# Two transformer blocks in one kernel: other buffers for a small MLP's weights, another instruction for 44 one-column sums, and 128 bytes between two groups of buffers

## The chip, the cores and the metric

The kernel runs on one core of one Trainium2 chip. The metric is the device time of one execution in microseconds. Five engines work beside each other, each on its own list of instructions: TensorE (PE in the rows; its weight loads are PEld), VectorE (DVE), ScalarE (ACT), GpSimd (POOL) and SyncE (SP, which here only issues DMAs).

## The reference, cut to what matters

256 tokens of width 1024, with 256 context tokens, go through two blocks. The first is attention in two forms, modulated by a small adaptive network, followed by a SwiGLU feed-forward with a hidden width of 2816:

```python
def _swiglu(h, w_ffn_in, w_ffn_out):
    gate, up = jnp.split(h @ w_ffn_in, 2, axis=-1)
    return (jax.nn.silu(gate) * up) @ w_ffn_out
...
    h = _modulate(_rmsnorm(new_lat), sh_f, sc_f)          # h * (1 + scale) + shift
    new_lat = new_lat + g_f * _swiglu(h, w_ffn_in, w_ffn_out)
```

The second block adds a state-space mixer (S5) and a sparse attention, merges them by gates, and ends in a squared-ReLU MLP with a hidden width of 4096. Its attention scores the queries against 15 compressed keys, which come out of a small MLP over blocks of 32 tokens (w1 is 2048x128 and w2 128x64, one pair for the keys and one for the values):

```python
def compress_blocks(tok, pe, w1, w2):
    ...
    return jax.nn.gelu(flat @ w1) @ w2
...
    kc = rmsnorm(compress_blocks(kv[0, 0], cmp_pe_k, cmp_wk1, cmp_wk2), k_norm_g[0])
    sc = jnp.einsum('bghqd,bgcd->bghqc', qb, kc) * scale - slopes * dist_c
...
        x = x + jnp.square(jax.nn.relu(h2 @ w_up[l])) @ w_down[l]
```

## The kernel before, in words

**Weights.** The large weights lie in one stream, `in_wseq`, in the order in which they are used. SyncE loads it in granules of 128x2048 fp32 (1 MB) into three buffers with the tag `raw`. ScalarE rounds each half of a granule to fp32r (`hi<-raw`, 128x1024), and VectorE computes what the rounding lost (`lo<-raw,hi`, 128x1024). There are four `hi` and four `lo` buffers. A 128x128 weight then costs three matmuls (`lin`): hi with the rounded activation, hi with its remainder, lo with the rounded activation. That keeps fp32 accuracy.

**Order.** The program is first recorded, instruction by instruction, and then ordered by a list scheduler in the class `Rec`, which keeps one clock per engine and hands out buffers in their order. `Rec.issue` then lays out the buffers in SBUF and writes every instruction; since that is one line, every row of the profile has the line L659 (L660 after the change). Tiles are told apart by their tags: `raw`, `hi`, `lo`; `c` for working tiles (20 of 128x256, made by `c1`, 32 of 128x512, made by `c2`, and 3 of 128x258, `c258`); `col` for a few columns; `xs` for the activations that the matmuls take; `mm`, `s`, `tp`, `v`, `la` for PSUM.

**Feed-forward in** ("ffi" below; the loop over 22 `j`, two `z` each). Each of the 44 lins takes 24 matmuls of 258 columns: 256 tokens, and two columns of the modulation's shift, rounded part and remainder. VectorE scales the PSUM result into a `c258` tile `t` and adds the tile's last column to the one before it, which gives one value per partition. ScalarE uses that of the gate as the bias of Silu, VectorE that of the up branch in the product. In the same stage VectorE and GpSimd compute row sums for the adaptive network (`raw<-raw,k_crow`), and GpSimd builds tables for the S5 mixer (`s5_params`).

**Feed-forward out** ("ffo") is 8 lins of 66 matmuls with 256 columns, whose activations are `c2` tiles.

**Second block.** After the projections come the compression MLP (`tp<-...`, 16 steps for each of keys and values), the S5 steps (`v<-k_cst,c`, `tp<-c,c`), the gate lins, and the scores against the compressed keys (`s<-k_crow,k_kcn`), which need the compression's result `k_kcn`. The compression's weights `w1` are two loads of 1 MB (`in_w` in the rows) into two of the three `raw` buffers, where they stay until the 32 matmuls have read them. At the end stand `up` (32 lins of 24 matmuls) and `down` (8 of 96).

**Addresses.** `Rec.issue` places buffers whose width is a multiple of 128 bytes first, pads the `xs` tiles, then 64 bytes, then all `hi` and `lo` buffers without a gap, then the rest.

Of the kernel before, what the change touches and what calls it, by code (L numbers as in the profile page):

```python
# [15 lines left out]
OP = mybir.AluOpType  # L16
# [338 lines left out]
class Rec:  # L355
# [276 lines left out]
    def issue(self):  # L632
        self.prepare()
        order = self.schedule()

        wide = {}
        for tops in self.tops:
            for r in tops:
                if r.tag in self.bufs and r.tag not in PSTAGS:
                    wide[r.tag] = max(wide.get(r.tag, 0), int(np.prod(r.shape[1:])))  # L640
        lay = [(f"{t}s{k}", w, None) for t, w in wide.items() for k in range(self.bufs[t])]
        lay += [(r.tag, int(np.prod(r.shape[1:])), r) for r in self.fixed]
        mid = [x for x in lay if x[0][:2] in ("hi", "lo")]
        whole = [x for x in lay if x[1] % 32 == 0 and x not in mid]

        small = [[x for x in lay if 0 < x[1] - lo <= 8] for lo in (8, 0)]
        for x in lay:
            if x[0][:2] == "xs":
                whole += [x] + [s.pop() if s else ("k_pad" + x[0], n, None) for s, n in zip(small, (16, 8))]
        rest = [x for x in lay if x not in whole and x not in mid]  # L650
        for tag, w, r in whole + [("k_pad", 16, None)] + mid + rest:
            if r is None:
                self.touch("lay_" + tag, tag, w)
            else:
                r.get()
        val = lambda x: x.get() if isinstance(x, View) else x
        for i in order:
            o = self.ops[i]
            getattr(self.real[o.eng], o.fn)(*[val(x) for x in o.args], **{k: val(x) for k, x in o.kw.items()})  # L659
# [6 lines left out]
def build(tc, nc, A, out):  # L666
    with ExitStack() as ctx:
        with tc.manual_schedule():
            _build(ctx, tc, nc, A, out)


def _build(ctx, tc, nc, A, out):
# [7 lines left out]
    V, ACT, G, PE, SP = (rec.eng(e) for e in ("V", "ACT", "G", "PE", "SP"))  # L680

    def own(pool, name, tag, shape, dt):

        def make():
            t = f"{tag}s{v.root.slot}"
            return pool.tile(shape, dt, tag=t, name=name, bufs=1)
        v = rec.root(tag, shape, dt, make)
        return v

    def T(tag, shape, dt=F32):  # L690
        cnt[0] += 1
        name = f"{tag}_{cnt[0]}"
        return own(sp, name, tag, shape, dt)
# [7 lines left out]
    def PS(tag, shape):  # L701
        cnt[0] += 1
        name = f"{tag}_{cnt[0]}"
        return own(pp, name, tag, shape, F32)
# [4 lines left out]
    def mm2(o, a, b, start, stop):  # L709
        return PE.matmul(o, a, b, start=start, stop=stop, skip_group_check=True)  # L710
# [3 lines left out]
    def PSR(shape, tags):  # L714
        k = rot[tags] = rot.get(tags, -1) + 1
        return PS(tags[k % len(tags)], shape)
# [4 lines left out]
    def c1(dt=F32, n=256):  # L721
        return T("c1", [128, n], dt)

    def c2(dt=F32):
        return T("c2", [128, 512], dt)
# [223 lines left out]
    def lin(o, base, nk, xh, xl, first=0, total=None, k0=0):  # L949

        total = total or nk
        for kc in range(nk):
            wh, wl = wt(base + kc)
            i = first + kc
            h, l = xh(kc), xl(kc)
            mm2(o, wh, h, i == 0, False)
            mm2(o[:, 0:_free(l)], wh, l, False, False)
            mm2(o, wl, h, False, i == total - 1)

    def split(dst_h, dst_l, src):  # L960
        ACT.activation(dst_h, src, AF.Copy)
        V.tensor_tensor(dst_l, src, dst_h.bitcast(F32), OP.subtract)
# [5 lines left out]
    def gemv(i):  # L968
        w = T("raw", [128, 2048])
        SP.dma_start(w, A["ada2"][i])  # L970
        for z in range(2):
            wz = w[:, 1024 * z:1024 * z + 1024]
            o = adc[i // 4][:, 2 * i % 8 + z:2 * i % 8 + z + 1]
            if z in GEMV_POOL[i]:
                G.tensor_tensor(wz, wz, crow, OP.mult)
                ACT.activation(wz, wz, AF.Copy, accum_out=o)
            else:
                V.tensor_tensor_reduce(wz, wz, crow, 1.0, 0.0, OP.mult, OP.add, o)
        if i % 4 == 3:
            o = adc[i // 4]  # L980
            V.tensor_tensor(o, o, col("b_ada", 16 + 2 * i - 6, 8), OP.add)
            if i == 11:
                V.tensor_scalar(o, o, 1.0, None, op0=OP.add)
# [74 lines left out]
    ps = fp[0]  # L1058
# [19 lines left out]
    for m in range(2):  # L1078
        t = c1()
# [7 lines left out]
    for m in range(4):  # L1087
        ps = fp[3 + m]
# [258 lines left out]
    for m in range(8):  # L1347
        if m < 4:
            ps = woa[m // 2][:, m % 2]
        else:  # L1350
            ps = PSR([128, 256], ("s", "v5", "s"))
# [6 lines left out]
                               op0=OP.mult, op1=OP.subtract)  # L1358
# [128 lines left out]
    for j in range(22):  # L1487
        ts = []
        for z in range(2):
            ps = PSR([128, 258], LIN)  # L1490
            lin(ps, BASE["ffi"] + 16 * j + 8 * z, 8, xh_, xl_)
            t = T("c258", [128, 258])
            V.tensor_tensor(t, ps, rsf, OP.mult)
            V.tensor_tensor(t[:, 256:257], t[:, 256:257], t[:, 257:258], OP.add)
            ts.append(t)
        a = c1()
        ACT.activation(a, ts[0][:, 0:256], AF.Silu, bias=ts[0][:, 256:257])
        V.scalar_tensor_tensor(a, ts[1][:, 0:256], ts[1][:, 256:257], a, op0=OP.add, op1=OP.mult)
        h_ = c2(F32R)
        split(h_[:, 0:256], h_[:, 256:512], a)  # L1500
        hid.append(h_)
        if j in (2, 6, 10, 14):
            gemv(12 + j // 4)
        if j == S5P_AT:
            sb2, cp, ca, dd, gd, TB = s5_params()
# [4 lines left out]
    for m in range(8):  # L1510
        ps = PSR([128, 256], LIN)
# [5 lines left out]
                               op0=OP.mult, op1=OP.subtract)  # L1517
# [25 lines left out]
    def lin2(base, tag="mm"):  # L1543
        ps = PS(tag, [128, 256])
        lin(ps, base, 8, xh2, xl2)
        return ps
# [9 lines left out]
    for m in range(4):  # L1556
        ps = lin2(BASE["u"] + 8 * m, UT[m])
# [4 lines left out]
        w_ = table[m]  # L1562
# [83 lines left out]
    TT = []  # L1646
    pe = T("col", [128, 32])
    SP.dma_start(pe, A["pe"])
    for z, nm in enumerate(("k0", "v0")):
        ps = lin2(BASE[nm], IN2[z])  # L1650
# [8 lines left out]
        t = c2().rearrange("p (a b) -> p a b", a=16)  # L1659
# [19 lines left out]
    for z, nm in enumerate(("k1", "k2")):  # L1679
        ps = lin2(BASE[nm], IN2[2 + z])  # L1680
# [31 lines left out]
    for m in range(4):  # L1712
        ps = lin2(BASE["q"] + 8 * m, QT[m])
# [13 lines left out]
    SP.dma_start(w2c, A["w2c"])  # L1727
    kcn, vcn = K("kcn", [128, 32]), K("vcn", [16, 2, 64])
    G.memset(kcn, 0.0)
    w1 = [T("raw", [128, 2048]) for _ in range(2)]  # L1730
    for z in range(2):
        SP.dma_start(w1[z], A["w1"][z])

    ps = PS("tp", [64, 128])
    for l2 in range(16):
        for z in range(2):
            mm2(ps[32 * z:32 * z + 32], TT[z][:, l2], w1[z][:, 128 * l2:128 * l2 + 128], l2 == 0, l2 == 15)
    hd, hx = c1(n=128)[0:64], c1(n=128)[0:64]
    V.tensor_copy(hx, ps)
    gelu_arg(hd, hx)  # L1740
# [28 lines left out]
    for g in range(2):  # L1769
        ps = PS("s", [128, 256])  # L1770
# [3 lines left out]
    for qt in range(2):  # L1774
# [24 lines left out]
        for g in range(2):  # L1799
# [3 lines left out]
            t = c2()  # L1803
# [27 lines left out]
        for kt in range(qt + 1):  # L1831
            for br in range(2):
                n_ += 1
                ts = []
                for g in range(2):
# [3 lines left out]
                    t = c2()  # L1839
# [16 lines left out]
    for q in range(4):  # L1856
        ACT.activation(ys[q], ys[q], AF.Gelu_apprx_tanh)
        t = c2(F32R)
# [9 lines left out]
    for m in range(4):  # L1868
        ps = PSR([128, 256], LIN)
        lin(ps, BASE["glu"] + 4 * m, 4, lambda kc: ygp[kc][:, 0:256], lambda kc: ygp[kc][:, 256:512])  # L1870
        t = c1()
# [9 lines left out]
    for m in range(8):  # L1881
# [9 lines left out]
        t = c2(F32R)  # L1891
# [3 lines left out]
    for m in range(8):  # L1895
        ps = PSR([128, 256], LIN)
# [15 lines left out]
    for j in range(32):  # L1912
        ps = PSR([128, 256], LIN)
# [8 lines left out]
    for m in range(8):  # L1922
        ps = PSR([128, 256], LIN)
        lin(ps, BASE["down"] + 32 * m, 32, lambda kc: hid[kc][:, 0:256], lambda kc: hid[kc][:, 256:512])
        t_ = c1()
        for z in range(2 if m == 7 else 1):
            c = slice(128 * z, 128 * z + 128) if m == 7 else slice(0, 256)
            t = t_.kid((slice(None), c))
# [18 lines left out]
```

## Time and profile before

| | |
|---|---|
| median of 3 runs | 813.47 us (812.05 to 814.28) |
| profiled execution | 813.07 us, its span 811.3 us (1.8 us lie around it) |
| mean granted TensorE clock | 0.976 of full speed |
| busy: PE, DVE, ACT, POOL | 773.4, 586.0, 433.0, 303.5 us |
| chain that ended last | PE 86%, DVE 8%, ACT 2%, DMA 2% |

Busy time says how full an engine is over the whole span. The chain follows the work back from the last instruction, at each step to whatever released it, so its shares tell which engine set the pace, and for how long.

### The profile page before, as it was taken

The page shows a single profiled execution, that of the slowest core. Times are in us where ns is not written, and L with a number is a line of the kernel's source. Part 1 is how long each engine was busy: PE and PEld are TensorE (multiplying, and loading weights), DVE is VectorE, ACT ScalarE, POOL GpSimd, SP SyncE. Part 2 cuts the span into 40 slices and gives each one's busy share as a digit, 9 for nine tenths or more (in the row PEclk, how much of TensorE's full clock was granted, in tenths as well). Part 3 has the DMA queues.
Part 4 walks back from the last instruction along what each step waited for, and adds up shares of the span by engine and source line. Part 5 has one row for each costly group of instructions (what it writes and reads, how often), then busy time and mean ns, then how long its engine had stood idle before and what let it go on. Part 6 is the DMA issues. An engine that isn't in the chain of part 4 may idle for free.

```text
span 811.3 us, 15419 instructions
## 1 busy us (share of the span) xinstructions
PE 773.4 (95%) x6063; PEld 699.5 (86%) x6063; DVE 586.0 (72%) x1156; ACT 433.0 (53%) x790; POOL 303.5 (37%) x320
## 2 busy tenths in 40 slices
PE   5999998999999898899999969999999999999998
PEld 3778775669999798899999857597999999999997
DVE  6678788787998899766676798656688655554552
ACT  6344549877654353465544323666646666643331
POOL 0015255680397999100002566785240333310000
PEclk9999899999999999999999995999999999999999
DMA  8955544435884464465556222033455545555540
GB/s 334 375 178 210 201 155 136 151 119 208 236 279 161 172 212 153 167 232 189 181 190 215 88 104 105 1 134 128 156 178 186 193 173 206 165 201 201 187 170 14
DMA packets 33131, 142.90 MB, mean 176 GB/s; under 512 B 11681, under 2 KB 15137, under 8 KB 16674
## 3 DMA queue, kind: packets, MB, share of 16 engines
q1 hardware_dynamic: 33058, 141.91, 49.8%
q8 instruction: 48, 0.79, 0.4%
q14 instruction: 25, 0.20, 0.1%
HBM read 139.53 MB, written 1.05 MB: 173 GB/s over the span
## 4 chain that ended last, share of the span: by engine, by line
PE 86%; DVE 8%; ACT 2%; DMA 2%; issue 1%; POOL 0%; SPq 0%; DVEq 0%; POOLq 0%
PE mm L659 41%; PE s L659 32%; PE tp L659 6%; DVE c L659 4%; PE la L659 4%; PE v L659 3%; DVE lo L659 2%; ACT c L659 1%; DMA raw<-in_wseq 1%; DVE col L659 1%; DMA raw<-in_ada 1%; ACT hi L659 0%; DMA k_X<-in_x 0%; POOL c L659 0%; DVE k_adc L659 0%
## 5 line engine op out<-in xcount | busy, mean ns | idle before, releaser
L659 DVE TENSOR_TENSOR lo<-raw,hi 128x1024 fp32r<-128x1024 f32 x206 | 258.6, 1258 | 98.7 <-ACT hi L659 97.6
L659 ACT ACTIVATE hi<-raw 128x1024 fp32r<-128x1024 f32 x206 | 215.6, 1050 | 193.5 <-PE mm L659 92.9
L659 PE MATMUL mm<-xs,hi 128*128 128x256 f32 (+1 forms) x992 | 187.9, 288 | 0.8 <-ACT hi L659 0.8
L659 PEld LDWEIGHTS mm<-xs,hi 128*128 128x128 f32 x992 | 156.5, 193 | 6.2 <-issue 4.2
L659 PE MATMUL mm<-c,hi 128*128 128x256 f32 (+1 forms) x744 | 144.3, 292 | 4.6 <-DVE c L659 2.6
L659 PE MATMUL mm<-xs,lo 128*128 128x256 f32 (+1 forms) x496 | 143.2, 289 | 2.6 <-DVE lo L659 2.5
L659 PEld LDWEIGHTS mm<-c,hi 128*128 128x128 f32 x744 | 115.9, 190 | 14.2 <-issue 4.7
L659 PE MATMUL s<-xs,hi 128*128 128x256 f32 (+1 forms) x672 | 124.7, 285 | 2.5 <-ACT hi L659 2.0
L659 PE MATMUL s<-c,hi 128*128 128x256 f32 (+1 forms) x676 | 122.7, 281 | 0.0
L659 PE MATMUL mm<-c,lo 128*128 128x256 f32 (+1 forms) x372 | 107.2, 290 | 1.3 <-DVE lo L659 1.2
L659 PEld LDWEIGHTS s<-xs,hi 128*128 128x128 f32 x672 | 104.3, 190 | 3.8 <-ACT hi L659 3.4
L659 PEld LDWEIGHTS s<-c,hi 128*128 128x128 f32 x676 | 104.0, 188 | 1.4 <-issue 0.4
L659 PEld LDWEIGHTS mm<-xs,lo 128*128 128x128 f32 x496 | 95.9, 194 | 5.1 <-DVE lo L659 4.3
L659 PE MATMUL s<-xs,lo 128*128 128x258 f32 (+1 forms) x336 | 95.9, 285 | 3.9 <-DVE lo L659 3.9
L659 ACT ACTIVATE c<-c 128x256 fp32r<-128x256 f32 (+4 forms) x141 | 61.7, 448 | 67.6 <-DVE c L659 64.5
L659 PE MATMUL s<-c,lo 128*128 128x256 f32 x338 | 95.1, 282 | 0.0
L659 POOL TENSOR_TENSOR raw<-raw,k_crow 128x1024 f32<-128x1024 f32 x18 | 46.3, 2576 | 102.2 <-DMA raw<-in_ada 101.8
L659 DVE TENSOR_TENSOR c<-c,c 128x256 fp32r<-128x256 f32 (+2 forms) x115 | 62.7, 558 | 20.3 <-POOL c L659 15.8
L659 POOL TENSOR_TENSOR c<-c 128x256 f32<-128x256 f32 x40 | 40.7, 1017 | 95.3 <-ACT c L659 81.8
L659 PEld LDWEIGHTS mm<-c,lo 128*128 128x128 f32 x372 | 71.5, 193 | 3.1 <-DVE lo L659 2.0
L659 PEld LDWEIGHTS s<-xs,lo 128*128 128x128 f32 x336 | 64.1, 191 | 4.9 <-DVE lo L659 4.8
L659 PEld LDWEIGHTS s<-c,lo 128*128 128x128 f32 x338 | 64.3, 190 | 0.4
(259 smaller groups left out, 1153.4 us busy)
## 6 DMA issues: line engine op xcount, KB each, us to landing
raw<-in_wseq SPq DMA_DIRECT2D x102, 1024.0 KB, 4.9
raw<-in_ada SPq DMA_DIRECT2D x20, 1024.0 KB, 5.0
tab<-in_ada SPq DMA_DIRECT2D x4, 1024.0 KB, 7.2
raw<-in_w SPq DMA_DIRECT2D x2, 1024.0 KB, 5.0
k_X<-in_x SPq DMA_DIRECT2D x4, 256.0 KB, 4.3
raw<-in_wseq SPq DMA_DIRECT2D x2, 512.0 KB, 7.5
tab<-in_ctx SPq DMA_DIRECT2D x4, 256.0 KB, 10.3
out<-c SPq DMA_DIRECT2D x7, 128.0 KB, 1.7
```

Source lines behind the costliest of these rows:

```text
L659: getattr(self.real[o.eng], o.fn)(*[val(x) for x in o.args], **{k: val(x) for k, x in o.kw.items()})
```

## The change

Three edits. The sum of the two shift columns becomes a `tensor_scalar`, whose second operand is a column read once per partition, in place of a `tensor_tensor` with two tensors. The weights `w1` get eight working tiles of 128x512 (`c2`) and are loaded by eight DMAs of 256 KB. The layout places all `hi` buffers, then 128 bytes of padding, then all `lo` buffers; `hi` stays where it was, and `lo` and all that follows move by 128 bytes.

```diff
@@ Rec.issue
-        mid = [x for x in lay if x[0][:2] in ("hi", "lo")]
+        mid = [x for t in ("hi", "lo") for x in lay if x[0][:2] == t]
+        mid.insert(self.bufs["hi"], ("k_pad2", 32, None))
@@ feed-forward in
             V.tensor_tensor(t, ps, rsf, OP.mult)
-            V.tensor_tensor(t[:, 256:257], t[:, 256:257], t[:, 257:258], OP.add)
+            V.tensor_scalar(t[:, 256:257], t[:, 257:258], t[:, 256:257], None, op0=OP.add)
@@ compression
-    w1 = [T("raw", [128, 2048]) for _ in range(2)]
+    w1 = [[c2() for _ in range(4)] for _ in range(2)]
     for z in range(2):
-        SP.dma_start(w1[z], A["w1"][z])
+        for i, w_ in enumerate(w1[z]):
+            SP.dma_start(w_, A["w1"][z][:, 512 * i:512 * i + 512])
...
-            mm2(ps[32 * z:32 * z + 32], TT[z][:, l2], w1[z][:, 128 * l2:128 * l2 + 128], l2 == 0, l2 == 15)
+            mm2(ps[32 * z:32 * z + 32], TT[z][:, l2], w1[z][l2 // 4][:, 128 * (l2 % 4):128 * (l2 % 4) + 128], l2 == 0, l2 == 15)
```

The scheduler orders the program anew. Three places show it.

SyncE's list, from the last granules of ffo on. `raw_...<-in_wseq` is a granule, `in_w` is w1, `k_cst<-c` are small tiles for the S5 steps. Before:

```order
L659 DMA raw_4802<-in_wseq 128x2048
L659 DMA raw_4876<-in_wseq 128x2048
...
L659 DMA raw_5242<-in_w 128x2048
...
L659 DMA raw_5329<-in_w 128x2048
...
L659 DMA raw_5371<-in_wseq 128x2048
...
L659 DMA raw_5580<-in_wseq 128x2048
L659 DMA c_924_5595<-in_w2c 128x128
L659 DMA raw_5770<-in_wseq 128x2048
```

After:

```order
L660 DMA raw_4803<-in_wseq 128x2048
L660 DMA c_925_4868<-in_w 128x512
L660 DMA c_926_4876<-in_w 128x512
L660 DMA raw_4882<-in_wseq 128x2048
L660 DMA c_927_4890<-in_w 128x512
...
L660 DMA c_932_4919<-in_w 128x512
L660 DMA raw_4952<-in_wseq 128x2048
...
L660 DMA raw_5259<-in_wseq 128x2048
...
L660 DMA raw_5346<-in_wseq 128x2048
...
L660 DMA raw_5388<-in_wseq 128x2048
...
L660 DMA raw_5499<-in_wseq 128x2048
L660 DMA c_924_5618<-in_w2c 128x128
```

The loads of w1 moved ahead, into the end of ffo, and two granules (`raw_5259` and `raw_5346`) now stand where the two loads of w1 stood.

TensorE's list at the compression. `tp<-raw` or `tp<-c_92x, c_93x` are its matmuls, `mm<-xs,hi` and `mm<-xs,lo` those of a gate lin, `v` and `tp<-k_cst` S5 steps and a transpose, `s<-k_crow,k_kcn` the scores. Before, from the last compression matmul:

```order
L659 MATMUL tp_5720<-raw_5329,c_844_4861 32x128
L659 MATMUL v_941_5768<-k_cst,c_555_3398 128x128
...
L659 MATMUL v_978_5828<-k_cst,c_557_3493 128x128
L659 MATMUL tp_5847<-k_cst,c_928_5786 128x64
...
L659 MATMUL s_5882<-k_crow,k_kcn 32x256 x4
L659 MATMUL s_5890<-k_crow,k_kcn 32x256 x4
L659 MATMUL mm_5671<-xs_4322,lo_5888 128x256
L659 MATMUL mm_5671<-xs_4419,hi_5656 128x256 x2
```

After:

```order
L660 MATMUL tp_5741<-c_932_4919,c_844_4862 32x128
...
L660 MATMUL mm_5797<-xs_4323,hi_5515 128x256 x2
L660 MATMUL mm_5797<-xs_4323,lo_5584 128x256
...
L660 MATMUL mm_5797<-xs_4970,lo_5584 128x256
L660 MATMUL mm_5865<-xs_4323,hi_5551 128x256 x2
L660 MATMUL mm_5879<-xs_4323,hi_5630 128x256 x2
...
L660 MATMUL tp_5891<-k_cst,c_934_5808 128x64
...
L660 MATMUL s_5929<-k_crow,k_kcn 32x256 x4
```

A whole gate lin (24 matmuls) and four matmuls of two more now stand between the compression and the scores; before, only two of the lin `mm_5671` were done by then, and the third waits behind the scores for `lo_5888`, a half of a granule that is loaded after the compression.

VectorE's list in ffi, around the tile `c_584`. `c<-mm,k_rsf` and `c<-s,k_rsf` read PSUM; `128x1` is the sum of the two columns; the other rows read two tiles of SBUF. Before:

```order
L659 TENSOR_TENSOR c_584_3176<-mm_3131,k_rsf 128x258
L659 TENSOR_TENSOR lo_3184<-raw_2915,hi_3056 128x1024
L659 TENSOR_TENSOR c_580_3182<-c_579_3155,c_580_3182 128x256
L659 TENSOR_TENSOR c_584_3176<-c_584_3176 128x1
L659 TENSOR_TENSOR lo_3214<-raw_2915,hi_3098 128x1024
L659 TENSOR_TENSOR c_589_3221<-s_3168,k_rsf 128x258
L659 TENSOR_TENSOR c_589_3221<-c_589_3221 128x1
L659 TENSOR_TENSOR lo_3234<-raw_2989,hi_3133 128x1024
```

After:

```order
L660 TENSOR_TENSOR lo_3148<-raw_2923,hi_3100 128x1024
L660 TENSOR_TENSOR c_584_3175<-mm_3135,k_rsf 128x258
L660 TENSOR_SCALAR c_584_3175<-c_584_3175 128x1
L660 SCALAR_TENSOR_TENSOR c_579_3115<-c_578_3140,c_579_3115 128x256
L660 TENSOR_TENSOR c_589_3211<-s_3170,k_rsf 128x258
L660 TENSOR_SCALAR c_589_3211<-c_589_3211 128x1
L660 TENSOR_TENSOR c_580_3200<-c_579_3115,c_580_3200 128x256
L660 SCALAR_TENSOR_TENSOR c_590_3188<-c_589_3211,c_590_3188 128x256
L660 TENSOR_TENSOR c_595_3254<-mm_3208,k_rsf 128x258
```

The sum still follows its PSUM read, but the `lo` rows stand elsewhere, and behind each sum there is still a row that reads two tiles of SBUF.

## Rows read from the trace of the kernel before

**Rows 1.** The page: busy us, share of the span, instructions.

```profile
PE 773.4 (95%) x6063; PEld 699.5 (86%) x6063; DVE 586.0 (72%) x1156; ACT 433.0 (53%) x790; POOL 303.5 (37%) x320
```

**Rows 2.** Windows: from:to, length; busy PE, PEld, DVE, ACT, POOL; clock, DMA share, GB/s.

```profile
256.00:346.00 90.00, 80.68 (x679) 77.68 (x678) 77.58 (x109) 39.61 (x57) 70.17 (x60) 0.96 0.49 174
346.00:410.00 64.00, 64.00 (x566) 64.00 (x564) 42.07 (x61) 35.72 (x51) 0.26 (x2) 1.00 0.56 198
470.00:490.00 20.00, 14.04 (x186) 10.40 (x185) 19.11 (x50) 4.60 (x11) 14.86 (x25) 0.89 0.28 106
490.00:507.00 17.00, 17.00 (x111) 13.23 (x113) 14.92 (x73) 7.13 (x29) 9.65 (x17) 0.53 0.36 125
```

**Rows 3.** Waits of PE, 255 to 350: us in total, times, longest.

```profile
PE s L659 <- DVE lo L659: 3.4, 3, 2.2
PE mm L659 <- DVE lo L659: 2.5, 3, 1.3
```

**Rows 4.** Groups of DVE by shape, 195 to 350: busy us, mean ns.

```profile
L659 DVE TENSOR_TENSOR lo<-raw,hi 128x1024 fp32r<-128x1024 f32 x48 | 63.1, 1322 | 1.6 <-ACT hi L659 1.5
L659 DVE TENSOR_TENSOR c<-c 128x1 f32<-128x1 f32 x43 | 19.1, 450 | 0.1
```

**Rows 5.** Timeline of DVE in ffi: start, us.

```profile
262.27 1.25 DVE L659 TENSOR_TENSOR c<-c 128x1 f32<-128x1 f32 x1
263.43 1.21 DVE L659 TENSOR_TENSOR lo<-raw,hi 128x1024 fp32r<-128x1024 f32 x1
...
302.17 1.07 DVE L659 TENSOR_TENSOR c<-c 128x1 f32<-128x1 f32 x2
303.17 2.08 DVE L659 TENSOR_TENSOR lo<-raw,hi 128x1024 fp32r<-128x1024 f32 x1
...
326.76 1.32 DVE L659 TENSOR_TENSOR c<-c 128x1 f32<-128x1 f32 x2
```

**Rows 6.** Timeline of POOL over the same stretch.

```profile
262.14 1.36 POOL L659 TENSOR_TENSOR c<-c,c 128x512 f32<-128x512 f32 x1
...
301.92 1.23 POOL L659 TENSOR_TENSOR tab<-tab,col 128x512 f32<-128x512 f32 x1
303.12 1.04 POOL L659 TENSOR_TENSOR c<-tab,col 128x512 f32<-128x512 f32 x1
```

**Rows 7.** Groups of DVE by shape, whole span: one-tensor operations.

```profile
L659 DVE TENSOR_SCALAR c<-c,col 128x512 f32<-128x512 f32 x12 | 10.7, 900 | 0.1
...
L659 DVE TENSOR_SCALAR col<-col 128x1 f32<-128x1 f32 x32 | 4.5, 147 | 0.2
...
L659 DVE TENSOR_SCALAR k_neg<-k_abi 128x16 f32<-128x16 f32 x1 | 1.0, 1023 | 0.0
```

**Rows 8.** Timeline of all engines, 163.7 to 164.4.

```profile
163.87 2.61 POOL L659 TENSOR_TENSOR raw<-raw,k_crow 128x1024 f32<-128x1024 f32 x1 [4.16 <-DMA raw<-in_ada]
164.18 0.15 DVE L659 TENSOR_SCALAR col<-col 128x1 f32<-128x1 f32 x1
```

**Rows 9.** Timeline of SP's queue, 430 to 480: start, us to issue.

```profile
432.12 0.33 SPq L659 DMA_DIRECT2D raw<-in_w  x1
...
476.98 0.80 SPq L659 DMA_DIRECT2D raw<-in_wseq  x2
```

**Rows 10.** The chain that ended last, 465 to 490: start, us, what.

```profile
473.24 3.90 PE tp L659 x66
...
477.40 6.85 DMA raw<-in_wseq
```

**Rows 11.** The same chain: one step each of ffi, ffo, up and down.

```profile
323.58 2.88 PE mm L659 x24
...
402.22 7.48 PE s L659 x66
...
714.12 2.83 PE s L659 x24
...
784.78 11.31 PE mm L659 x96
```

## Prediction

> **What bounds the kernel now.** The page's first part comes first: TensorE is busy for 773.4 of 811.3 us [rows 1], so only some 38 us can come from its waiting; all else must come from its speed. The windows by stage say where it waits and where it is slow [rows 2]. In ffo it is never idle, at full clock. Between 256 and 346, in ffi, it is idle for 90 − 80.68 = 9.3 us, and the granted clock of 0.96 (two levels, 2.4 and 1.2 GHz) costs another 0.04 × 90 = 3.6 us: 12.9 us in all. Between 470 and 490 it is idle for 6.0 us, and it spends the 17 us behind that at a clock of 0.53, near the lower level.
>
> The waits say for whom. In ffi it is above all `lo`, the second half of a weight, which VectorE makes: 3.4 + 2.5 us [rows 3]. VectorE is busy for 77.6 of those 90 us and GpSimd for 70.2 [rows 2]. At 470 to 490 the chain of waits shows the compression's matmuls (66 with two of the S5 steps), and then a granule of weights that is loaded only once w1 lets go of its `raw` buffer: 6.85 us from 477.40 [rows 10]. The load stands in SyncE's queue at 476.98; w1 had its first buffer since 432.12 [rows 9].
>
> **The sum of two columns.** 43 of the 44 lie in ffi and take 19.1 us, 450 ns each [rows 4]. One-column `TENSOR_SCALAR`s take 147 ns, the mean of 32 [rows 7]. So 43 × 0.303 = 13.0 us of VectorE time are at stake. Why 450? At 262.27 the sum takes 1.25 us and ends at 263.5, just when GpSimd's operation, begun at 262.14, does [rows 5, 6]. The one-column operation at 164.18 takes 0.15 us inside one of GpSimd's 2.61 us [rows 8]. So the sum waits because it reads two tensors of SBUF, and the new form should not: I put it at 0.15 us. A one-tensor operation isn't safe by itself, though: at 512 columns the mean is 900 ns, and one of 16 columns took 1,023 ns [rows 7].
>
> The Trainium skill, "SBUF — State Buffer", section "Who interferes with whom", has both sides: two SBUF inputs contend with a GpSimd operation that reads SBUF, and whoever comes second waits for all of it; a `tensor_scalar` can also enter a mode with both ports and then contends too. By the second half the new form would save nothing; the 147 ns speak against that for one column, but those 32 take constants, not a column of SBUF, as second operand.
>
> But is the wait gone, or passed on? The `lo` split reads two tensors too. At 303.17 it takes 2.08 us instead of the 1.21 of 263.43, since GpSimd's operation of 303.12 runs until 304.16 [rows 5, 6]. Take the sum at 262.27 away: `lo` then stands there at 262.4, waits for the same end at 263.5, and ends where it did. Along VectorE's timeline in ffi there are 15 sums of over 0.5 us. Behind 11 of them the next instruction reads two SBUF tensors, as here; behind 2 VectorE idles anyway. Two are left. At 302.17 two sums end with GpSimd's operation, at 303.2; GpSimd then gets the next turn, and `lo` waits a second time, 2.08 − 1.21 = 0.87 us. With the sums out of the way `lo` would be first in line. At 326.76 two sums take 1.32 us and a PSUM read follows, which no port holds: 1.32 − 0.2 = 1.1 us. So about 2 of the 13 us are really saved, and the order after the change has the same form, a reader of two tensors soon behind each sum. What is late next is that reader. Of the 2 us, the 0.87 lies before a wait of TensorE; of the other I count half. **−1.5 us.** Bounds: 12.9 us gained, all idle and slow time of the stage; or 1.7 lost, if the new order loses two turns of 0.87.
>
> **w1 in working tiles.** Two `raw` buffers are no longer held from 432 to 477, and two more granules come before the compression, so a gate lin and four matmuls more stand between it and the scores, 28 where there were 2. At 11.31/96 = 117.8 ns [rows 11] the 26 are worth 3.1 us of the 6.0 us of idle time, work that is later done at the cost of the path. Against that, their `lo` split, 1.21 us [rows 5], may fall into a stage where VectorE has 19.11 of 20 us taken [rows 2]; as the granule comes earlier, it may also be done before. I charge half: **−2.5 us.** The best case adds the clock: if the fuller stretch keeps it from falling, the 17 us shrink toward 9, but VectorE's 14.92 us of work there allow only 2.1; 5.2 in all. The worst: the lin fills nothing, and the split costs 1.2.
>
> The loads move into ffo's end: 2 MB. There 198 GB/s fill 0.56 of the DMA engines [rows 2], so full speed is about 354 GB/s, and 2 MB take some 5.9 us of the 28 that are free. A granule lasts 48 matmuls, 48 × 7.48/66 = 5.4 us [rows 11], with three buffers in turn. The 1.5 MB that stand right before `raw_4952` may make it 4.4 us late, less than one granule's use; I put it at nothing. If a granule's lead weren't there, 4.4 us would be the price. SyncE's issues cost 0.33 us each [rows 9]; six more than before, 2 us, lie under the same lead. The matmuls are unchanged.
>
> **128 bytes.** What could depend on it is TensorE's rate, since a matmul reads an activation while weights for the next are loaded. Two rates stand in the rows for the same operands at full clock: ffo 7.48/66 = 113.3 ns, up and down 2.83/24 = 11.31/96 = 117.8 [rows 11]. All these weights lie in the same `hi` and `lo` buffers, so addresses alone don't decide it, and the trace doesn't say what does. If `lo`'s new place brought the 1,920 matmuls from the gate and output projections through up and down (768 each) to the better rate, 1,920 × 4.5 ns = 8.6 us would be gained; if each third matmul, the one on `lo`, cost 4.5 ns more, up to 6,063/3 × 4.5 = 9.1 us [rows 1] lost, and with 3,504 matmuls of ffi, ffo, up, down and the projections alone 5.3. Nothing in the rows favours a sign: **0**. VectorE reads `hi` and writes `lo`; its undisturbed split takes 1.21 us for 1,024 columns where one column takes 0.15, about 1.04 ns a column, a steady stream, and I count no gain there.
>
> The Trainium skill, same page and section, gives TensorE two read ports of its own and says that it never waits on anyone. By that the pad is worth 0 too. The two rates show that something does make a difference.
>
> **Sum.** 813.07 − 1.5 − 2.5 = 809.1 for the profiled execution; the median of the runs is 0.4 above that one, so 809.3, say **809 us**. With the likeliest case's own spread, 806 to 811.
>
> **Rivals.**
> *The port wait vanishes.* For it: 13.0 us of waiting in a stage with 12.9 to recover, and a sum that is quick lets ScalarE's Silu begin earlier. Against it: the eleven waits above have an heir. At 8 us of gain, between 1.5 and 12.9, the time is 802.5. Chance 0.12.
> *The closing stages take the better rate.* For it: ffo holds it through 528 matmuls; against: nothing but that they didn't before. 809.1 − 8.6 = 800.5. Chance 0.17.
> *The `lo` matmuls get slower.* The mirror image, one mechanism, and the one that ends on the other side: 4.5 ns on each matmul whose weight is in `lo`. From some 1,000 of them on (4.4 us) the two gains are gone, from 1,500 (6.8 us) the kernel is slower by over 0.3%. At 7, between 5.3 and 9.1: 816. Chance 0.20.
> *Neither edit pays.* The new sum waits like the old one, or its wait is always passed on; and the fuller hole is paid back by VectorE, or `raw_4952` is late. For it: VectorE is the busy engine in both places. 812.5, at most 815. Chance 0.18.
> The forecast itself keeps 0.33.
>
> **Numbers.** 0.3% (2.4 us) is about what a measurement of this kernel tells from no change. Faster than 811.0: most of the forecast (0.27), the first two rivals (0.29) and a little of the last, 0.58. Within: the rest of the forecast, a third of the third rival, most of the last, 0.25. Slower: 0.17. The range from 800 to 816.5 leaves out half of the better rate's case and the worse half of the third rival, some 0.18.
>
> **What would show it.** The 44 sums as `TENSOR_SCALAR` at about 0.15 us, GpSimd running or not; if they take 0.4, the form waits. The `lo` splits and two-tensor operations of ffi longer on average than 1,322 ns: then the wait was passed on; if they stay there and PE's waits on `lo` (5.9 us) fall below 2, it vanished. At the compression: 24 `mm` matmuls ahead of the scores, PE's idle time there down from 6.0 to about 3, and no granule in the chain. In ffo no idle time; `raw` loads before the compression not in the chain. The steps of 66 and 96 matmuls at 7.48 and 11.31 us; any other figure there is the pad's, and it alone would make the forecast wrong by more than its own spread.

## The result, and the profile after

The changed kernel takes 800.99 us in the median of 4 runs (798.59 to 801.71), the kernel before 812.76 beside it. The ratio is 0.9837, with a 95% interval of 0.9805 to 0.9869: 13 us faster by the ratio, 11.8 by the medians. That is the sign of the forecast and inside its range, but about three times the 4.0 us that its terms add up to. The profiled execution took 800.42 us, its span 798.4. Times are medians of all runs of a kernel; ratios and mean clocks leave out the few runs that took over 1.5% more than the fastest of their kernel.

The page of the changed kernel answers to [rows 1]: busy us, share, instructions.

```profile
PE 761.0 (95%) x6063; PEld 688.7 (86%) x6063; DVE 582.9 (73%) x1156; ACT 432.4 (54%) x790; POOL 303.5 (38%) x320
```

TensorE does the same 6,063 matmuls in 12.4 us less busy time. Nearly the whole gain is matmuls that run faster, not waits that are gone. They do so in two ways. One is the clock: the mean granted clock of the four runs is 0.985, where before's runs beside the experiments average 0.977 to 0.980. By these shares of 800 us the clock gives 4 to 6 us, an estimate that counts time at the lower level as half lost. The other is a faster rate at the same clock. The chain of the changed kernel shows that one, beside [rows 11]; the columns are start, us, what.

```profile
399.21 7.48 PE s L660 x66
...
574.30 1.36 PE s L660 x12
...
667.72 2.83 PE mm L660 x24
...
772.59 10.88 PE mm L660 x96
```

ffo and up are as before. The steps of 12 matmuls, of the gate and output projections, took 1.41 us in the chain of before and take 1.36; down went from 11.31 to 10.88 per 96, that is from 117.8 to 113.3 ns a matmul. The last step of ffo ends at 406.7 instead of 409.7 (3.0 us, the part from ffi and ahead of it; between 256 and 346 the clock is 0.98 instead of 0.96, worth 1.8 of them); down's first step begins 9.7 us earlier than in before's chain (707.29 against 716.94), and the span ends 12.9 us earlier. So 6.7 us came between ffo and down, and 3.2 in down.

In ffi, VectorE's groups, over the same 195 to 350 as [rows 4]; busy us, mean ns. Two rows of before that [rows 4] lack, then those after:

```profile
L659 DVE TENSOR_TENSOR c<-c,c 128x256 fp32r<-128x256 f32 x21 | 13.2, 626 | 2.9 <-ACT c L659 2.8
L659 DVE CUSTOM_DVE_ANT_0 raw<-raw,k_crow 128x1024 f32<-128x1024 f32 x5 | 6.1, 1219 | 0.0
```

```profile
L660 DVE TENSOR_TENSOR lo<-raw,hi 128x1024 fp32r<-128x1024 f32 x48 | 67.0, 1411 | 1.1 <-ACT hi L660 1.0
L660 DVE TENSOR_TENSOR c<-c,c 128x256 fp32r<-128x256 f32 x21 | 17.7, 842 | 2.9 <-ACT c L660 2.9
...
L660 DVE TENSOR_SCALAR c<-c 128x1 f32<-128x1 f32 x44 | 9.3, 211 | 0.9
...
L660 DVE CUSTOM_DVE_ANT_0 raw<-raw,k_crow 128x1024 f32<-128x1024 f32 x5 | 8.7, 1747 | 0.0
```

The sums fell from 19.1 to 9.3 us, and the readers of two tensors took most of that over: the `lo` splits rose from 63.1 to 67.0, the products from 13.2 to 17.7 and the row sums from 6.1 to 8.7 (a fourth group of them fell, from 15.5 to 13.2). One place shows how. VectorE's timeline, then GpSimd's:

```profile
279.75 2.63 DVE L660 TENSOR_TENSOR c<-c,c 128x256 fp32r<-128x256 f32 x1
282.30 0.20 DVE L660 TENSOR_SCALAR c<-c 128x1 f32<-128x1 f32 x1
```

```profile
279.70 2.39 POOL L660 TENSOR_TENSOR raw<-raw,k_crow 128x1024 f32<-128x1024 f32 x1
282.05 0.65 POOL L660 TENSOR_TENSOR tab<-tab,c 128x128 f32<-128x128 f32 x1
```

The product at 279.75 waits until GpSimd's long operation ends at 282.1. The sum at 282.30 begins and ends inside the next one. PE's waits on `lo` in the stage hardly changed beside [rows 3]:

```profile
PE s L660 <- DVE lo L660: 4.5, 4, 2.4
PE mm L660 <- DVE lo L660: 2.0, 3, 1.2
```

At the compression, the windows beside [rows 2] (busy PE, PEld, DVE, ACT, POOL; clock, DMA share, GB/s), and the chain beside [rows 10]:

```profile
470.00:490.00 20.00, 16.66 (x180) 13.39 (x179) 18.27 (x50) 4.70 (x13) 15.36 (x24) 0.84 0.01 2
490.00:507.00 17.00, 16.86 (x128) 12.82 (x129) 13.79 (x79) 8.40 (x36) 12.92 (x20) 0.68 0.36 125
```

```profile
470.57 4.09 PE tp L660 x68
...
475.30 1.72 PE mm L660 x13
...
479.06 1.39 PE mm L660 x10
...
486.84 1.12 PE s L660 x16
```

PE's idle time at 470 to 490 fell from 6.0 to 3.3 us, the gate lin's matmuls stand in the chain where the granule stood, and the clock over the 17 us behind that rose from 0.53 to 0.68 (over the 20 us themselves it fell from 0.89 to 0.84). SyncE's queue shows the loads of w1 at the end of ffo:

```profile
400.31 0.80 SPq L660 DMA_DIRECT2D c<-in_w  x2
...
401.64 4.07 SPq L660 DMA_DIRECT2D c<-in_w  x6
406.30 6.51 SPq L660 DMA_DIRECT2D raw<-in_wseq  x2
```

The next granule is issued 4.7 us behind them at 406.30, and ffo still has no idle time.

### The profile page after: what moved, and what is told of

Its sections match the earlier page's. It is cut to its first block, busy times and chain, and to the rows that moved or that the text cites. A ratio compares the mean times of both kernels' runs of the same rounds, so it can differ in the third digit from the quotient of the medians.

```text
span 798.4 us, 15427 instructions
## 1 busy us (share of the span) xinstructions
PE 761.0 (95%) x6063; PEld 688.7 (86%) x6063; DVE 582.9 (73%) x1156; ACT 432.4 (54%) x790; POOL 303.5 (38%) x320
## 4 chain that ended last, share of the span: by engine, by line
PE 82%; DVE 9%; DMA 2%; ACT 2%; POOL 2%; issue 1%; SPq 0%; DVEq 0%; POOLq 0%; ACTq 0%
PE mm L660 39%; PE s L660 31%; PE tp L660 6%; DVE c L660 5%; PE la L660 4%; PE v L660 3%; DVE lo L660 3%; DMA raw<-in_ada 1%; ACT c L660 1%; DMA raw<-in_wseq 1%; DVE col L660 1%; ACT hi L660 1%; POOL c L660 1%; POOL tab L660 0%; POOL col L660 0%
## 5 line engine op out<-in xcount | busy, mean ns | idle before, releaser
L660 PE MATMUL mm<-xs,hi 128*128 128x256 f32 (+1 forms) x992 | 185.0, 285 | 2.3 <-ACT hi L660 1.2
L660 PEld LDWEIGHTS mm<-xs,hi 128*128 128x128 f32 x992 | 153.2, 189 | 7.3 <-issue 3.4
L660 PE MATMUL mm<-c,hi 128*128 128x256 f32 (+1 forms) x744 | 140.3, 287 | 4.7 <-DVE c L660 2.7
L660 PE MATMUL mm<-xs,lo 128*128 128x256 f32 (+1 forms) x496 | 140.7, 284 | 2.0 <-DVE lo L660 2.0
L660 PEld LDWEIGHTS mm<-c,hi 128*128 128x128 f32 x744 | 113.7, 188 | 13.8 <-DVE c L660 4.4
L660 PE MATMUL s<-c,hi 128*128 128x256 f32 (+1 forms) x676 | 120.6, 280 | 1.1 <-ACT hi L660 1.1
L660 PE MATMUL mm<-c,lo 128*128 128x256 f32 (+1 forms) x372 | 105.3, 284 | 1.3 <-DVE lo L660 1.2
L660 PEld LDWEIGHTS mm<-xs,lo 128*128 128x128 f32 x496 | 93.8, 189 | 4.3 <-DVE lo L660 2.6
L660 DVE TENSOR_TENSOR c<-c,c 128x256 fp32r<-128x256 f32 (+2 forms) x115 | 67.3, 598 | 19.8 <-POOL c L660 15.7
L660 PEld LDWEIGHTS mm<-c,lo 128*128 128x128 f32 x372 | 69.7, 188 | 3.1 <-DVE lo L660 1.7
```

## The experiments

All ratios are to runs of the kernel before on the same chip, with a 95% interval.

**Each edit alone, and all but the gap.** Each takes its part of the diff.

> Only the 128 bytes between hi and lo; the order of the instructions is that of before. Theory (the address of lo sets TensorE's rate): the steps of 96 matmuls in down fall from 11.31 to 10.88 us and those of the gate and output projections from 117.8 to 113.3 ns a matmul, so 5 to 6 us are gained, ratio about 0.993; ffo stays at 7.48 us per 66. Rival (which of the two rates a stage takes is set by what ran ahead of it, a stall or a switch of activations, and the address has no part): with the old order the old rates stay, 11.31 us per 96, ratio 1.000 within 0.003.

Measured: 808.47 us, ratio 0.9912 (0.9877 to 0.9946). Its chain:

```profile
401.89 7.48 PE s L660 x66
...
583.71 1.36 PE s L660 x12
...
697.02 2.83 PE mm L660 x24
...
735.76 10.88 PE mm L660 x96
```

The 128 bytes alone, with every instruction in its old place, give the faster rate in the projections and in down, and not in up; ffi's steps rise from 2.88 to 2.91 us. The steps in the chain account for some 5 of the 7 us, which lies inside the interval.

> The changed kernel without the 128 bytes, its order kept. Theory (the address sets the rate): down is back at 11.31 us per 96, the gate and output projections at 117.8 ns, and the kernel some 5 to 6 us slower than with the pad: ratio to before about 0.991. Rival (the order sets the rate): down stays at 10.88 us per 96 and the ratio at about 0.984, that of the changed kernel.

Measured: 806.94 us, 0.9909 (0.9878 to 0.9941). Its chain has the old steps, 1.41 and 11.31. The rate belongs to the gap, not to the new order.

> Only the 44 sums as one-tensor operation, and the order that the scheduler makes of it. Theory (the wait for the port is passed on): the sums take about 0.2 us, the lo splits and two-tensor operations of that stage get longer, ffo begins 1 to 2.5 us earlier, ratio 0.997 to 0.999; the scores and what lies behind them are unchanged. Rival (the wait vanishes, but later stages hid it in the changed kernel): ffo begins 5 us earlier or more, ratio 0.994 or below. Rival on the rates: if the order alone sets them, down's steps of 96 move to 10.88 us here too, 3.4 us more.

Measured: 808.64 us, 0.9938 (0.9907 to 0.9968). In its chain ffo's first step begins at 347.21, in before's at 349.84, 2.6 us later. VectorE's groups over 195 to 350: the sums 9.3 us (210 ns each), the `lo` splits 68.8 and the row sums 10.7. So most of the wait is passed on, as the first theory says, but the ratio lies between the two theories, below the 0.997 that the first one allowed.

> Only the compression's weights in working tiles. Theory: the interval from ffo's start to a matmul count of 1,000 behind it shrinks by about 5 us as in the changed kernel, of which some 3 are the 20 to 26 matmuls that fill the hole ahead of the scores and the rest is less time at the lower clock; ratio about 0.994; down stays at 11.31 us per 96. Rival (the filler is paid back, and the 5 us are the pad's through a faster rate in those lins): 1 to 2 us, ratio 0.998, with the stretch at the lower clock as long as before (17 to 20 us).

Measured: 810.19 us, 0.9961 (0.9932 to 0.999). Its windows:

```profile
470.00:490.00 20.00, 15.99 (x178) 12.22 (x178) 18.68 (x49) 4.79 (x14) 14.10 (x26) 0.90 0.01 2
490.00:507.00 17.00, 16.82 (x102) 11.87 (x102) 13.36 (x60) 6.05 (x25) 12.55 (x16) 0.52 0.37 124
```

2.0 us more of matmuls in the hole, and the clock behind it as low as before. Part of the filler is paid back: behind the scores a `lo` split of 1.15 us (490.79) now stands in the chain, ahead of the gate lins. The ratio lies between the theory and the rival. Without the gap but with both other edits, the same stretch has 0.69 (first row). But this is one execution of each kernel. ts_only and tt_new_order (below), which both have the old loads of w1 and the same list of instructions on every engine, show 0.50 and 0.68 there (second and third row):

```profile
490.00:507.00 17.00, 16.68 (x128) 12.69 (x129) 14.16 (x79) 7.91 (x34) 12.29 (x18) 0.69 0.34 125
490.00:507.00 17.00, 17.00 (x111) 13.46 (x112) 11.13 (x61) 6.99 (x25) 8.64 (x15) 0.50 0.35 124
490.00:507.00 17.00, 17.00 (x126) 13.46 (x126) 12.83 (x70) 8.77 (x34) 9.15 (x15) 0.68 0.35 125
```

So these rows don't show which edit the better clock there belongs to.

The three ratios multiply to 0.981, and all three at once measured 0.9837 (0.9805 to 0.9869): within the intervals, the gains add.

**The new sum or its new order.** The scheduler counts on a port that VectorE and GpSimd share in turns. It gives a one-column operation of two tensors a place in these turns, and a one-tensor operation none, so the edit also reorders. Two kernels, on before, separate this; the first has the new sum and the old order, the second the old sum and the new order. Both change what the scheduler takes the sum for:

```diff
+        if m == "tensor_scalar" and n == 1 and args[1].root.top().tag == "c258":
+            m = "tensor_tensor"
```

```diff
+        if m == "tensor_tensor" and n == 1 and args[1].root.top().tag == "c258":
+            m = "tensor_scalar"
```

> Before with the new sum, but scheduled as if it were the old one, so that all engines keep their order. Theory (the wait is passed on to the next reader of two tensors): sums at 0.21 us, VectorE's busy time over the stage within 1 us of before, ffo begins 0.5 to 2 us earlier, ratio 0.997 to 1.000, so that the rest of what the one-edit kernel gained (0.994) is the new order's. Rival (the instruction itself is the gain): ratio 0.994 here too, ffo 2.5 us earlier.

Measured: 813.63 us, 0.9986 (0.9951 to 1.0022). Its groups:

```profile
L661 DVE TENSOR_TENSOR lo<-raw,hi 128x1024 fp32r<-128x1024 f32 x50 | 67.4, 1355 | 2.6 <-ACT hi L661 2.4
...
L661 DVE CUSTOM_DVE_ANT_0 raw<-raw,k_crow 128x1024 f32<-128x1024 f32 x5 | 8.5, 1696 | 0.0
L661 DVE TENSOR_SCALAR c<-c 128x1 f32<-128x1 f32 x43 | 8.5, 204 | 0.1
```

The sums no longer wait, the `lo` splits take 1,355 ns instead of 1,322, and the row sums 8.5 us instead of 6.1. In its chain ffo's first step begins at 349.54, 0.3 us earlier than in before's, less than either theory had.

> The counterpart of the run with the new sum in the old order: the old two-tensor sums in the order that the scheduler makes for the new ones; every engine's list is that of the kernel with the new sum alone. Theory (the gain of 0.994 is the new order's, since the wait is passed on): ratio 0.993 to 0.996, ffo begins near 347 us, sums at 0.4 us. Rival (the two need each other: the new order counts on sums that do not wait): ratio 0.998 to 1.003, ffo at 349 us or later.

Measured: 811.03 us, 0.9962 (0.9935 to 0.999). Its sums wait as ever:

```profile
L661 DVE TENSOR_TENSOR c<-c 128x1 f32<-128x1 f32 x44 | 21.0, 477 | 0.9
```

The instruction alone isn't told from no change, at 10.6 us of VectorE time saved on the sums; the order alone is a gain. In the second kernel's chain ffo's first step begins at 347.91, 1.9 us earlier than in before's. Such starts are those of one execution: ffi itself begins at 210.41 in before, 214.24 in ts_old_order and 211.64 in tt_new_order, and its clock from 256 to 346 is 0.96 in the first and 1.00 in the other two, worth 3.6 us. So the means of all runs say more. What the order gains is the clock, as far as the runs tell. The mean granted clock is 0.9813 over the 12 runs with the new order alone, and 0.9777 in the 27 of before beside them (difference 0.0036, 95% interval 0.0005 to 0.0067). That is some 2.9 us of 811, an estimate as above, and the means of the times differ by 2.7. ts_only, with the same order, has 0.9818 against 0.9785; ts_old_order, with the old one, 0.9776 against 0.9766. Why this order keeps a higher clock, the runs don't show.

**What the gap does.** Places are told as bytes modulo 256, from the layout: working tiles at 128, `hi` and `lo` at 192, `xs` tiles alternately at 128 and 0; the change moves `lo` to 64. Four layouts, each on before:

```diff
 both_moved
-        for tag, w, r in whole + [("k_pad", 16, None)] + mid + rest:
+        for tag, w, r in whole + [("k_pad", 48, None)] + mid + rest:
 gap_256
+        mid = [x for t in ("hi", "lo") for x in lay if x[0][:2] == t]
+        gap = [x for x in lay if x[0] in ("cols30", "cols31")]
+        mid[self.bufs["hi"]:self.bufs["hi"]] = gap
 gap_64
+        mid.insert(self.bufs["hi"], ("k_pad2", 16, None))
 flipped
+        for tag, w, r in (whole + [("k_pad", 16, None)] + mid[self.bufs["hi"] + 1:]
+                          + [("k_pad2", 32, None)] + mid[:self.bufs["hi"]] + rest):
```

> Before, with hi and lo both moved by 128 bytes and no gap between them; same order. Theory A (what counts is that hi and lo lie 128 bytes apart modulo 256): both still share their place, so the closing stages stay at 11.31 us per 96 and 117.8 ns a matmul, ratio 1.000 within 0.003. Theory B (lo's own place against the activations is what counts): down goes to 10.88 us per 96 or below and the ratio to 0.991 as with the gap. Rival C (the place of the buffers behind lo): like B.

Measured: 815.02 us, 1.001 (0.9976 to 1.0044). Down stays at 11.31, as theory A says; but ffo, too, takes the slow rate now, 7.77 us per 66, which no theory had. The buffers behind `lo` lie 128 bytes further here as in the change, so rival C is out.

> Before, with 256 bytes (two buffers of small columns) between hi and lo instead of 128, so that both start at the same place modulo 256. Theory (distance modulo 256 counts): down stays at 11.31 us per 96, the gate and output projections at 117.8 ns a matmul, ratio 1.000 within 0.003. Rival (any gap does it, since lo no longer follows hi directly): 10.88 us per 96 and a ratio of about 0.991.

Measured: 814.28 us, 1.0007 (0.9973 to 1.0042), every step as in before. A gap as such does nothing.

> Before with 64 bytes between hi and lo instead of 128. Theory (hi and lo must lie 128 bytes apart modulo 256, each 64 from the activations): at 64 lo lies 128 from the working tiles, neither as before nor as in the change; the closing stages do not get the 10.88 us per 96, ratio 0.998 or above, perhaps slower than before. Rival (any different place will do): 10.88 us and 0.991.

Measured: 816.64 us, 1.0036 (1.001 to 1.0062), a little slower than before: ffo takes 7.80 us per 66, down 11.35 per 96.

> Before with lo first, then 128 bytes, then hi: lo where it was, hi 128 bytes further modulo 256, the mirror image of the change. Theory (the distance of hi and lo counts, not which of them lies where): down at 10.88 us per 96, the gate and output projections at 113.3 ns a matmul, ratio 0.991 as with the pad alone. Rival (lo's own place counts): 11.31 us and a ratio of 1.000.

Measured: 815.51 us, 1.0022 (0.9994 to 1.005). Here my theory fell. The distance is there, `hi` and `lo` are only exchanged, and the chain shows the projections change their rate in the middle:

```profile
577.05 1.36 PE s L660 x12
578.41 6.97 PE mm L660 x60
585.38 1.43 PE s L660 x12
...
787.28 11.41 PE mm L660 x96
```

The 60 matmuls contain a gate lin, whose activations are `xs` tiles. Ahead of it the projections, on working tiles, run at 113.3 ns, behind it at about 119 (1.43/12), and so does all of down (11.41/96 = 118.9). That pointed at the `xs` tiles. The next four kernels place them all alike, two on before, xs_same on the changed kernel, and xs_nopad on the changed kernel without its gap; buffers of 128 bytes go between them, so that no other tile changes its place modulo 256 (for 0 instead of 128, one more ahead of the first).

```diff
             if x[0][:2] == "xs":
                 whole += [x] + [s.pop() if s else ("k_pad" + x[0], n, None) for s, n in zip(small, (16, 8))]
+                whole += [y for y in whole if y[0] == f"cols{24 + int(x[0][3:])}"]
+                whole.remove(whole[-1])
```

> Before with all xs tiles at the same place modulo 256 and no gap between hi and lo. Theory (with hi and lo at the same place a stage can take either rate, as ffo and down do): up is no better for it, 2.83 us per 24, or by luck 2.72 throughout; down stays at 11.31; ratio 0.996 to 1.000. Rival (the alternation of xs alone slows up and then down behind it): up 2.72, down 10.88, ratio 0.985 to 0.990.

Measured: 802.54 us, 0.9875 (0.9833 to 0.9916). The rival won, without any gap:

```profile
220.52 2.85 PE mm L661 x24
...
583.31 1.36 PE mm L661 x12
...
703.45 2.72 PE mm L661 x24
...
730.65 10.88 PE mm L661 x96
```

> Before with all eight xs tiles at the same place modulo 256, but 128 bytes from the working tiles, where the run with xs alone had them on the working tiles' place. Theory D1 (it is the alternation from one matmul to the next): up and the second block's input run at 113.3 ns here too, and down behind them, ratio 0.985 to 0.990. Theory D2 (it is the place of an activation against the weights: 64 bytes behind them good, 64 ahead bad): the xs stages run at 117.8 ns or more and hand it on to down, ratio 0.998 or above.

Measured: 811.72 us, 0.9993 (0.9963 to 1.0023). No alternation, and no gain: the alternation isn't needed for the slow rate, and the place counts. Whether it is the place against the weights or against the working tiles, this run doesn't tell.

```profile
399.90 7.48 PE s L669 x66
...
706.57 2.83 PE mm L669 x24
```

> The changed kernel with all eight xs tiles (the activations of ffi, of the second block's input and of up) at the same place modulo 256 as the working tiles, where they alternate by 128 bytes now. Theory (the rate is set by where activations and weights lie modulo 256): up goes from 2.83 to 2.72 us per 24 and ffi, with 258 columns, from 2.90 to about 2.75, so up gives 3.4 us, the projections 1 to 2, and ffi up to 4 where VectorE lets it; ratio to before 0.973 to 0.980. Rival (the alternation of xs has no part, up's rate is set by its stall at the beginning): 2.83 us per 24 as before and the ratio of the changed kernel, 0.984.

Measured: 793.47 us, 0.9748 (0.9711 to 0.9785), below the changed kernel's interval. Up takes 2.72 us per 24, the projections 1.36 per 12; ffi stays at 2.88, not 2.75 as I had expected.

> The changed kernel without the 128 bytes between hi and lo, but with all xs tiles at one place modulo 256. Theory D (the alternating xs tiles bring a stage into the slow rate, and the stages behind inherit it; the gap only lets them leave it): nothing is left for the gap to do, 113.3 ns a matmul from the second block's input to down, ffi at 118.5 ns as with the xs tiles alone, ratio 0.972 to 0.978, as with both. Rival E (the gap has a gain of its own): slower than with both, ratio 0.980 or above.

Measured: 795.61 us, 0.9768 (0.9737 to 0.9798), so the first theory's range, though not all of its reason: the projections kept the slow rate, and up left it.

```profile
578.94 1.41 PE mm L661 x12
...
697.88 2.72 PE mm L661 x24
...
725.08 10.88 PE mm L661 x96
```

The steps of all layouts, each the commonest in its stage of the chain, in us, from the one profiled execution of each kernel. The five other kernels with before's places (no_pad, ts_only, w1_only, ts_old_order, tt_new_order) have before's steps, so a step is no accident of one execution:

| kernel | xs | hi | lo | ffi x24 | ffo x66 | projections x12 | up x24 | down x96 |
|---|---|---|---|---|---|---|---|---|
| before, gap_256 | 128, 0 | 192 | 192 | 2.88 | 7.48 | 1.41 | 2.83 | 11.31 |
| pad_only, the change | 128, 0 | 192 | 64 | 2.91 | 7.48 | 1.36 | 2.83 | 10.88 |
| both_moved | 128, 0 | 64 | 64 | 2.88 | 7.77 | 1.41 | 2.80 | 11.31 |
| gap_64 | 128, 0 | 192 | 0 | 2.87 | 7.80 | 1.42 | 2.83 | 11.35 |
| flipped | 128, 0 | 64 | 192 | 2.91 | 7.48 | 1.43 | 2.77 | 11.41 |
| xs_at0 | 0 | 192 | 192 | 2.83 | 7.48 | 1.41 | 2.83 | 11.31 |
| xs_only | 128 | 192 | 192 | 2.85 | 7.48 | 1.36 | 2.72 | 10.88 |
| xs_nopad | 128 | 192 | 192 | 2.85 | 7.48 | 1.41 | 2.72 | 10.88 |
| xs_same | 128 | 192 | 64 | 2.88 | 7.48 | 1.36 | 2.72 | 10.88 |

Three things stand in it. With all operands of a stage in the same places, both rates occur: before's ffo and down, or the projections of xs_only and xs_nopad. With `xs` at 0 and `hi`, `lo` at 192, up is slow, and down behind it stays slow. And with `hi` at 192 and `lo` at 64 the stages on working tiles are fast in all three kernels that have it, also behind `xs` tiles that alternate; with both at 64 (both_moved) they are slow.

## Why the prediction was right or wrong

**The 128 bytes: the step that failed.** I had both rates in the rows [rows 11], priced the better one for the closing stages at 8.6 us, and took 0, since "nothing in the rows favours a sign". The gap alone gave 0.9912, about 7.2 us of 813.96, and that is most of what the forecast missed. The rival with that price was the right one, but up stayed out of it. That its 800.5 us came so near the measured 800.99 is in part luck: it counted 3.5 us of up, which gained nothing, and left out the clock, worth about 5 (estimate above). What I read past: down ran at the slow rate on the very places on which ffo ran at the better one, so the slow rate was nothing that those places had to have, and a change of them could free down from it; that down had more to win than ffo to lose was in the rows. The sign itself hung on more than I could read there: mirrored, the gap gives 1.0022, and none of the other three ways of moving the weights gained anything.

The Trainium skill, "SBUF — State Buffer", section "Who interferes with whom", says that TensorE never waits on anyone. By it the gap would be worth nothing. Here down takes 113.3 ns a matmul in pad_only and 117.8 in before, with the same lists of instructions and a granted clock of 1.00 in both from 720 to 790 us; only the places of tiles differ. The measurement decides.

**The sum of two columns: the mechanism right, one term left out.** The quicker sums alone are worth little, as the step said: with the old order kept, 10.6 us of the sums' time are gone and the ratio is 0.9986 (0.9951 to 1.0022), which fits the 1.5 us, and no gain as well. But the step went on that "the order after the change has the same form", and counted the new order as nothing. The order alone gave 0.9962, about 3 us, which the mean clock accounts for, and both together 0.9938, about 5. The sum itself takes 0.21 us, not 0.15; the 32 operations that I took it from have constants. The rule of the Trainium skill, in the section named above, that a `tensor_scalar` may also contend with GpSimd did not bite at one column: 211 ns on average, and 0.20 us at 282.30 beside GpSimd.

**w1: the size right, the working in part.** Forecast 2.5 us, alone about 3.2 (0.9961; 0.9932 to 0.999). The gate lin stands in the hole, PE's idle time there fell from 6.0 to 4.0 us by this edit alone and to 3.3 with all three, about as forecast, and the moved loads cost ffo nothing. The split that I had charged by half is in the chain. The clock, which I had only in the best case, may carry part of the gain: its mean is 0.9806 in w1_only against 0.9785, some 1.7 us, but the difference is within its noise (0.003). That no granule is in the chain shows nothing: in eight of the eleven kernels with the old loads it isn't there either (in pad_only VectorE's `c` steps stand in its place, from 477.40 on).

**The clock and the sum.** The sum had the clock's gain at nothing; by the estimate above it gave 4 to 6 of the 13 us. A slip besides: 809.1 and 0.4 make 809.5, not 809.3.

**The rivals.** The port wait didn't vanish. The `lo` matmuls didn't get slower in this layout. In others a stage did: ffo by 4.4 to 4.8 ns a matmul in both_moved and gap_64 (7.77 and 7.80), down by 0.4 to 1.0 in gap_64 and flipped (11.35 and 11.41), so a loss was a real possibility; whether it fell on the `lo` matmuls alone isn't shown.

**Open.** What in the chip makes the places matter, and why the same places can have either rate, no run shows; that a stage inherits its rate from the one ahead fits flipped, but xs_nopad's up left the slow rate that stood ahead of it. Also open is why the new order is granted a higher clock. Why no stage with 258 columns got below 2.83 us per 24 is open too.

## What to carry to other kernels

A layout edit is no null edit: before calling it one, look for two rates of the same matmul at the same clock in the trace, and ask where in the program the rate changes. When a scheduler orders the program, an instruction's cost in its tables is part of the edit: keep the order and change the instruction, then the reverse, and the two gains come apart. Compare the mean granted clock of all runs, too, before a gain of 0.4% is put down to waits. A wait for a shared port is worth what the next user of the port doesn't wait in its place.

## What the runs showed of the hardware that was not expected

The time of a 256-column matmul depends on where its activations and weights lie modulo 256 bytes: from 113.3 to 118.9 ns at full clock, kept over 768 matmuls in a row. It depends on more than that, since ffo and down of before have 113.3 and 117.8 with the same places. With `xs` tiles at the working tiles' place on top of the change, the kernel takes 793.47 us, ratio 0.9748, the fastest of all that ran.
